# Fresh and reloaded keys mixed two and two, and half of a float split moved to VectorE, in a three-stage transformer block

## The chip, the cores and the metric

The kernel runs on one core of a Trainium2 chip. The time is the device time of one launch in microseconds, the median of several runs. The engines are named as the profile names them: PE is TensorE (PEld its weight loads), DVE is VectorE, ACT is ScalarE, POOL is GpSimd, SP is SyncE, which here only issues DMAs.

## What is computed

A mixing block of gated linear attention and spatial gating comes first. Then a retrieval layer takes most of the time: each of 1024 tokens picks 8 x 16 of 16384 single-neuron experts and sums them.

```python
def peer(x, w_q, sub_k1, sub_k2, expert_u, expert_v):
    q = (xt @ w_q).reshape(T, 8, 2, 128)
    s1 = einsum('thd,kd->thk', q[:, :, 0], sub_k1); s2 = einsum('thd,kd->thk', q[:, :, 1], sub_k2)
    v1, i1 = top_k(s1, 16); v2, i2 = top_k(s2, 16)
    cand = (v1[..., :, None] + v2[..., None, :]).reshape(T, 8, 256)
    vals, ci = top_k(cand, 16)
    idx = take(i1, ci // 16) * 128 + take(i2, ci % 16)
    gates = softmax(vals)
    ...
        u = expert_u[ii]                      # 128 rows of 1024 for each token
        a = gelu(einsum('tkd,td->tk', u, xx)) * gg
        return einsum('tk,tkd->td', a, expert_v[ii])
```

## The kernel before

The 1024 tokens are 8 blocks of 128. Blocks 0 to 3 fetch their experts row by row, with indirect DMAs that POOL issues: `u_steps` gathers rows of `expert_u` and a dot product on DVE (L748) takes each; `v_steps` (two of the blocks) sums rows of `expert_v` on PE into `gacc` (L828); `v_rows` (the other two) adds them up on DVE into `racc` (L799). Blocks 4 to 7 are computed densely: a *key* is a group of 128 experts, and for each of the 128 keys the hidden values of all 512 tokens are a matmul against `expert_u` (`h_phase`, `hp`), times a gate that is zero for most, and a second matmul against `expert_v` (`v_phase`, `vp`). Precision is kept by splitting each float into a high and a low half (`uh`/`ul`, `vh`/`vl`, `ah`/`al`) and three matmuls per product.

The program has four stages. **Stage 0** is the front block with top-k and its decoding (`topk_steps`). **Stage 1** is gateless: `h_phase` runs for the first HEAD = 72 keys and stores the results in DRAM (`a_d`), while `gate_steps` builds the gates of the dense blocks (`gJ`, `gW`, `gp`, `gst`) and stores them as `g_d`. **Stage 2** takes all 128 keys. For one of the first 72 the hidden values are reloaded (`Ar`); for one of the other 56 they are computed afresh. `gates` loads the gates `G` of G2 = 4 neighbouring keys at a time, `gated` multiplies and splits on DVE and ACT (L993 to L995), `split` loads `expert_u` or `expert_v` (`rawu`, `rawv`), makes the high half on ACT (L927) and the low half on DVE for `u` (L929) or on POOL for `v` (L931). After each group of GI = 4 keys one `v_phase` of 96 matmuls adds them to the sums `dacc` (DVE, L1011). It is recorded behind the first key of the next group. **The tail** is what is left of `v_rows`.

In stage 2 four fresh or four reloaded keys form a group, in the order RFRFRFRRFRFRFRFRRFRFRFRRFRFRFRFR (R reloaded, F fresh). Thus between two `v_phase`s lie four `h_phase`s, or one, or three, or, where reloaded groups meet, none.

Gathers are woven in by `Queue`: after each piece of matmul work `pump` gives a queue credit in proportion (rates 0.7 and 0.4 in stage 1, 0.65 and 0.4 in stage 2), and a gathered row costs 1.4. `paced` makes a gather wait for the last matmul recorded. A scheduler then sets the order of each engine's instructions, and every engine works in that order. A dot product is recorded UAHEAD rows behind its gather, 4 in stages 0 and 1 and 2 in stage 2; the gathered rows rotate through 5 buffers `gu` and, up to the end of stage 1, GUX = 4 more (`gux`).

Of the kernel before, what the change touches and what calls it, by code (L numbers as in the profile page):

```python
# [67 lines left out]
def block_kernel(ctx: ExitStack, tc: tile.TileContext, a, out):  # L68
# [518 lines left out]
    def topk_steps(b, G):  # L587
# [49 lines left out]
        nh = 2  # L637
        for h0 in range(0, HEADS, nh):
            hk = slice(h0 * TOPK, (h0 + nh) * TOPK)
            for half in range(2):  # L640
                eq = tk.tile([P, nh, TOPK, TOPK], BF16, name="eq")
                sh = [P, nh * TOPK, TOPK]
                nc.vector.tensor_tensor(eq.rearrange("p h k j -> p (h k) j"),
                                        ab[:, half, hk].unsqueeze(2).to_broadcast(sh),
                                        iota_f.unsqueeze(1).to_broadcast(sh), op=ALU.is_equal)
# [19 lines left out]
    def gate_steps(gb, b):  # L665
# [10 lines left out]
        def product():  # L676
# [235 lines left out]
    def dense(pump):  # L912
        TP = TB // 2 if TB > 512 else TB
        NP = TB // TP
        with tc.tile_pool(name="dn", bufs=1) as dn, ExitStack() as dvx:
# [193 lines left out]
```

## Time and profile before

| | us |
|---|---|
| median of three runs | 3422.1 (3421.41 to 3426.11) |
| the profiled execution | 3430.3 |
| its span, first to last instruction | 3428.4 |
| PE busy in it | 2960.9 (86%) |
| DVE busy | 2636.7 (77%) |
| POOL busy | 1915.4 (56%) |
| ACT busy | 1075.9 (31%) |

Stage 1 begins at 1174 us, the last matmul of stage 1 ends at 1872, stage 2's matmuls begin at 1899 and the last `dacc` sum ends at 3315. A matmul's record is longer than the step to the next one, since they are pipelined, so a busy PE is not a full one.

### The profile page before, as it was taken

The page shows a single profiled execution, that of the slowest core. Times are in us where ns is not written, and L with a number is a line of the kernel's source. Part 1 is how long each engine was busy: PE and PEld are TensorE (multiplying, and loading weights), DVE is VectorE, ACT ScalarE, POOL GpSimd, SP SyncE. Part 2 cuts the span into 40 slices and gives each one's busy share as a digit, 9 for nine tenths or more (in the row PEclk, how much of TensorE's full clock was granted, in tenths as well). Part 3 has the DMA queues.
Part 4 walks back from the last instruction along what each step waited for, and adds up shares of the span by engine and source line. Part 5 has one row for each costly group of instructions (what it writes and reads, how often), then busy time and mean ns, then how long its engine had stood idle before and what let it go on. Part 6 is the DMA issues. An engine that isn't in the chain of part 4 may idle for free. (4 is left out here: it accounts for less than half of the span.)

```text
span 3428.4 us, 42728 instructions
## 1 busy us (share of the span) xinstructions
PE 2960.9 (86%) x14906; PEld 2324.4 (68%) x14906; DVE 2636.7 (77%) x4989; ACT 1075.9 (31%) x2000; POOL 1915.4 (56%) x1303
## 2 busy tenths in 40 slices
PE   8988999998877799999898898999999988888840
PEld 8988888987867676676574565555655676666730
DVE  5656897789997797997865666565656688999999
ACT  5444233342323354555451221122111222222210
POOL 0002467655665364454455656676666666677776
PEclk9999899999988899999999899999999999989975
DMA  5555367764556698999899988988888878898888
GB/s 178 164 190 148 108 197 234 251 207 151 184 191 205 211 403 324 335 369 352 327 392 386 348 293 289 328 312 307 299 311 312 315 270 279 288 326 301 298 307 337
DMA packets 344442, 944.98 MB, mean 276 GB/s; under 512 B 32913, under 2 KB 123281, under 8 KB 342178
## 3 DMA queue, kind: packets, MB, share of 16 engines
q0 software_dynamic: 147456, 536.94, 43.1%
q1 hardware_dynamic: 196770, 405.31, 35.1%
q8 instruction: 117, 1.92, 0.2%
q14 instruction: 99, 0.81, 0.1%
HBM read 868.72 MB, written 73.40 MB: 275 GB/s over the span
## 5 line engine op out<-in xcount | busy, mean ns | idle before, releaser
L759 POOL DMA_INDIRECT gu<-in_pu,ii x370 | 448.3, 1212 | 374.0 <-PE hp L946 145.4
L246 POOL TENSOR_TENSOR wlo<-wraw,whi 128x1024 fp32r<-128x1024 f32 x140 | 351.5, 2528 | 482.7 <-ACT whi L244 475.6
L748 DVE SCALAR_TENSOR_TENSOR gu<-gu,gn 128x1024 f32<-128x1024 f32 x370 | 548.9, 1501 | 64.7 <-DMA gu<-in_pu,ii 63.9
L1007 PE MATMUL vp<-vl,ah 128*128 128x512 f32 x1024 | 422.6, 414 | 67.3 <-POOL vl L931 67.2
L1006 PE MATMUL vp<-vh,ah 128*128 128x512 f32 x1024 | 401.4, 418 | 76.3 <-ACT vh L927 45.4
L944 PE MATMUL hp<-dnh,uh 128*128 128x512 f32 x1024 | 411.2, 402 | 32.1 <-ACT uh L927 28.7
L1008 PE MATMUL vp<-vh,al 128*128 128x512 f32 x1024 | 414.0, 408 | 2.6 <-DVE al L995 2.6
L946 PE MATMUL hp<-dnh,ul 128*128 128x512 f32 x1024 | 408.0, 399 | 5.9 <-DVE ul L929 5.8
L945 PE MATMUL hp<-dnl,uh 128*128 128x512 f32 x1024 | 407.4, 398 | 0.0
L842 POOL DMA_INDIRECT gv<-in_pv,iT x256 | 292.4, 1142 | 203.3 <-PE gacc L828 112.2
L931 POOL TENSOR_TENSOR vl<-rawv,vh 128x1024 fp32r<-128x1024 f32 x128 | 328.5, 2578 | 70.6 <-ACT vh L927 69.2
L1011 DVE TENSOR_TENSOR dacc<-dacc,vp 128x512 f32<-128x512 f32 x256 | 169.2, 683 | 237.8 <-PE vp L1008 237.6
L244 ACT ACTIVATE whi<-wraw 128x1024 fp32r<-128x1024 f32 x216 | 225.3, 1057 | 287.1 <-DMA wraw<-in_wt 83.7
L828 PE MATMUL gacc<-gv,wz 128*32 128x512 f32 x1024 | 312.3, 603 | 2.9 <-DMA gv<-in_pv,iT 2.7
L1006 PEld LDWEIGHTS vp<-vh,ah 128*128 128x128 f32 x1024 | 202.5, 200 | 165.4 <-ACT vh L927 56.8
L1007 PEld LDWEIGHTS vp<-vl,ah 128*128 128x128 f32 x1024 | 203.0, 198 | 140.2 <-POOL vl L931 85.0
L759 POOL DMA_INDIRECT gux<-in_pu,ii x142 | 177.9, 1253 | 198.3 <-PE hp L946 89.6
L944 PEld LDWEIGHTS hp<-dnh,uh 128*128 128x128 f32 x1024 | 194.0, 190 | 110.0 <-ACT uh L927 32.7
L803 POOL DMA_INDIRECT gr<-in_pv,ii x151 | 192.3, 1273 | 101.1 <-DVE racc L799 61.8
L1008 PEld LDWEIGHTS vp<-vh,al 128*128 128x128 f32 x1024 | 202.7, 198 | 58.4 <-issue 12.6
L946 PEld LDWEIGHTS hp<-dnh,ul 128*128 128x128 f32 x1024 | 193.8, 189 | 69.1 <-issue 18.4
L945 PEld LDWEIGHTS hp<-dnl,uh 128*128 128x128 f32 x1024 | 194.2, 190 | 61.4 <-issue 23.5
(273 smaller groups left out, 6798.3 us busy)
## 6 DMA issues: line engine op xcount, KB each, us to landing
rawu<-in_ut SPq DMA_DIRECT2D x128, 512.0 KB, 7.0
rawv<-in_pv SPq DMA_DIRECT2D x128, 512.0 KB, 5.3
wraw<-in_wt SPq DMA_DIRECT2D x120, 512.0 KB, 3.9
g_d<-gst SPq DMA_DIRECT2D x16, 2048.0 KB, 11.0
G<-g_d SPq DMA_DIRECT2D x128, 256.0 KB, 8.0
wraw<-in_wq SPq DMA_DIRECT2D x48, 512.0 KB, 4.4
a_d<-A SPq DMA_DIRECT2D x72, 256.0 KB, 7.4
Ar<-a_d SPq DMA_DIRECT2D x72, 256.0 KB, 5.8
```

What stands on the lines that cost most here:

```text
L246: eng.tensor_tensor(lo[:, :, sl], raw, hi[:, :, sl].bitcast(F32), op=ALU.subtract)
L748: queued(nc.vector.scalar_tensor_tensor(u, u, 1.0, n2, op0=ALU.mult, op1=ALU.mult, accum_out=hv[:, k:k + 1]), "dve")
L759: paced(nc.gpsimd.indirect_dma_start(out=u, out_offset=None, in_=a["pu"], in_offset=bass.IndirectOffsetOnAxis(ap=ii[:, k:k + 1], axis=0)))
L828: queued(nc.tensor.matmul(acc[32 * g:32 * g + 32, dh, :], z[:, g, 31 - r:63 - r], v[:, dh * 512:(dh + 1) * 512], start=r == 0, stop=r == 3 ...
L842: paced(nc.gpsimd.indirect_dma_start(out=v, out_offset=None, in_=a["pv"], in_offset=bass.IndirectOffsetOnAxis(ap=iTs[b][:, t:t + 1], axis=0)))
L931: nc.gpsimd.tensor_tensor(lo, raw, hi.bitcast(F32), op=ALU.subtract)
L944: nc.tensor.matmul(ps[:, :TP], uh[:, cs], nh[:, c, ts_], start=c == 0, stop=False)
L945: nc.tensor.matmul(ps[:, :TP], uh[:, cs], nl[:, c, ts_], start=False, stop=False)
L946: mm = nc.tensor.matmul(ps[:, :TP], ul[:, cs], nh[:, c, ts_], start=False, stop=c == DC - 1)
L1006: nc.tensor.matmul(ps, ah[:, bl], vh[:, ds_], start=x == 0, stop=False)
L1007: nc.tensor.matmul(ps, ah[:, bl], vl[:, ds_], start=False, stop=False)
L1008: mm = nc.tensor.matmul(ps, al[:, bl], vh[:, ds_], start=False, stop=x == n - 1)
```

## The change

- `order`: a group of four keys in stage 2 is now two fresh and two reloaded ones, HEAD is 64 (so 64 keys are reloaded and 64 fresh), and between two `v_phase`s there are always two `h_phase`s.
- Gates: G2 = 2 keys to a load, 4 buffers; GT = 64 tokens to a stored tile, so `g_d` is written in 8 pieces of 4 MB and not 16 of 2 MB, and `gst` has 2 buffers, not 3.
- `vl` is computed on DVE. The raw tiles have two buffers each; those of `u` lie in the pool `dn`, which lives through both dense stages.
- GUX 1, UAHEAD (3, 2).
- Decoding: four heads at a time, with the 16 choices as the outer and the results as the inner dimension, in a buffer shared with `cd`.

```diff
-HEAD = 72
+HEAD = 64
-GT = 32
-G2 = 4
+GT = 64
+G2 = 2
-RAWB = {"h": 3, "u": 2, "v": 2}
+RAWB = 2
-GUX = 4
+GUX = 1
-UAHEAD = (4, 2)
+UAHEAD = (3, 2)
...
-        nh = 2
+        nh = 4
...
-                eq = tk.tile([P, nh, TOPK, TOPK], BF16, name="eq")
...
-                                        ab[:, half, hk].unsqueeze(2).to_broadcast(sh),
-                                        iota_f.unsqueeze(1).to_broadcast(sh), op=ALU.is_equal)
-                nc.vector.tensor_tensor(eq, eq, xi[:, half, hk].rearrange("p (h j) -> p h j", h=nh).unsqueeze(2)
-                                        .to_broadcast([P, nh, TOPK, TOPK]), op=ALU.mult)
...
+                eq = tk.tile([P, TOPK, nh * TOPK], BF16, name="eq", tag="cd")
+                sh = [P, TOPK, nh * TOPK]
+                nc.vector.tensor_tensor(eq, ab[:, half, hk].unsqueeze(1).to_broadcast(sh),
+                                        iota_f.unsqueeze(2).to_broadcast(sh), op=ALU.is_equal)
+                e4 = eq.rearrange("p j (h k) -> p j h k", h=nh)
+                nc.vector.tensor_tensor(e4, e4, xi[:, half, hk].rearrange("p (h j) -> p j h", h=nh).unsqueeze(3)
+                                        .to_broadcast([P, TOPK, nh, TOPK]), op=ALU.mult)
+                nc.vector.tensor_reduce(yz[:, half, hk], eq.rearrange("p j k -> p k j"), axis=AX.X, op=ALU.add)
...
-                raw = raws[dst].tile([P, D], F32, name="raw" + dst, bufs=RAWB["h" if raws["u"] is not raws.get("v") else dst])
+                raw = pool.tile([P, D], F32, name="raw" + dst, bufs=RAWB)
...
-                if dst == "u":
-                    last["dve"] = nc.vector.tensor_tensor(lo, raw, hi.bitcast(F32), op=ALU.subtract).ins
-                else:
-                    nc.gpsimd.tensor_tensor(lo, raw, hi.bitcast(F32), op=ALU.subtract)
+                last["dve"] = nc.vector.tensor_tensor(lo, raw, hi.bitcast(F32), op=ALU.subtract).ins
...
-                    G = dv.tile([P, NB, P // GT, G2, GT], F32, name="G", bufs=2)
+                    G = dv.tile([P, NB, P // GT, G2, GT], F32, name="G", bufs=4)
...
-            pairs = sorted(range(P // G2), key=lambda n: (n + 0.5) / HEAD if n * G2 < HEAD
-                           else (n - HEAD // G2 + 0.5) / (P - HEAD))
-            order = [n * G2 + x for n in pairs for x in range(G2)]
+            order = [i for n in range(0, HEAD, G2) for h in (HEAD, 0) for i in range(h + n, h + n + G2)]
```

**Where stage 2 begins, on SP.** `dacc` is the sum, loaded with `h`; its buffers lie where stages 0 and 1 had theirs, so the first of these loads waits for the last gather and dot of stage 1. Before:

```order
L975 DMA dacc3_17456<-h_d7_98 128x1024
L1022 DMA Ar_17461<-a_d0_11327 128x512
L983 DMA G_17463<-g_d4_131 128x4x128
L983 DMA G_17463<-g_d5_132 128x4x128
L983 DMA G_17463<-g_d6_133 128x4x128
L983 DMA G_17463<-g_d7_134 128x4x128
L926 DMA rawv_17475<-in_pv 128x1024
L1022 DMA Ar_17479<-a_d1_11328 128x512
L926 DMA rawv_17488<-in_pv 128x1024
L926 DMA rawu_17520<-in_ut 128x1024
```

and with the change:

```order
L957 DMA a_d63_11342<-A_16864 128x512
L924 DMA rawu_17079<-in_ut 128x1024
L924 DMA rawu_17313<-in_ut 128x1024
L969 DMA dacc0_16917<-h_d4_95 128x1024
L969 DMA dacc1_16918<-h_d5_96 128x1024
L969 DMA dacc2_16919<-h_d6_97 128x1024
L969 DMA dacc3_16920<-h_d7_98 128x1024
L977 DMA G_16971<-g_d4_131 128x2x128
L977 DMA G_16971<-g_d5_132 128x2x128
L977 DMA G_16971<-g_d6_133 128x2x128
L977 DMA G_16971<-g_d7_134 128x2x128
L924 DMA rawv_16983<-in_pv 128x1024
```

Two loads of `rawu` now stand ahead of the first `dacc`; the third stands 24 loads behind it. PE's order has 72 `hp` matmuls (three keys) ahead of the first `vp`, where before it had two matmuls.

**In stage 2, the low half of v.** Before, on POOL, among the gathers (`gv`, `gu`), from the middle of the stage:

```order
L931 TENSOR_TENSOR vl_19045<-rawv_19046,vh_19044 128x1024
L842 DMA gv_18912<-in_pv,iT_18226 128x1024
L842 DMA gv_18931<-in_pv,iT_18226 128x1024
L759 DMA gu_18564<-in_pu,ii_16144 128x1024
L931 TENSOR_TENSOR vl_19104<-rawv_19105,vh_19103 128x1024
L759 DMA gu_18567<-in_pu,ii_16144 128x1024
```

and with the change on DVE, from the end of one `v_phase` interval to the next:

```order
L926 TENSOR_TENSOR ul_19366<-rawu_19367,uh_19365 128x1024
L987 TENSOR_TENSOR A_19051<-A_19051,G_19089 128x512
L989 TENSOR_TENSOR al_19095<-A_19051,ah_19094 128x512
L926 TENSOR_TENSOR vl_19027<-rawv_19028,vh_19026 128x1024
L926 TENSOR_TENSOR vl_19040<-rawv_19041,vh_19039 128x1024
L748 SCALAR_TENSOR_TENSOR gu_18428,hv_16006<-gu_18428,gn2_16004 128x1024
L748 SCALAR_TENSOR_TENSOR gu_18431,hv_16006<-gu_18431,gn2_16004 128x1024
L1005 TENSOR_TENSOR dacc0_16917<-dacc0_16917,vp_19099 128x512
```

POOL keeps the gathers alone. On DVE the third and fourth `vl` of a group stand behind the gate of the next group's first fresh key (A, al) and, elsewhere, between dots.

**Where the dense work ends, on DVE.** The last `dacc` sum and what follows it, before:

```order
L1011 TENSOR_TENSOR dacc3_17456<-dacc3_17456,vp_26755 128x512
L149 SCALAR_TENSOR_TENSOR rfr_26631<-rfq_26635,rfr_26631 128x1
L145 SCALAR_TENSOR_TENSOR rfq_26683<-rfr_26679,rfh_26681 128x1
L799 SCALAR_TENSOR_TENSOR racc_24195<-gv_25112,w_24192,racc_24195 128x1024
L145 SCALAR_TENSOR_TENSOR rfq_26635<-rfr_26631,rfh_26633 128x1
```

and with the change:

```order
L1005 TENSOR_TENSOR dacc3_16920<-dacc3_16920,vp_26739 128x512
L799 SCALAR_TENSOR_TENSOR racc_24131<-gr_24183,w_24128,racc_24131 128x1024
L145 SCALAR_TENSOR_TENSOR rfq_26619<-rfr_26615,rfh_26617 128x1
L145 SCALAR_TENSOR_TENSOR rfq_26667<-rfr_26663,rfh_26665 128x1
L164 TENSOR_SCALAR rfv_26757<-rfss_26754 128x1
L799 SCALAR_TENSOR_TENSOR racc_24131<-gv_24200,w_24128,racc_24131 128x1024
```

Behind the last `dacc` sum stand 75 adds of `racc` before, and 124 now.

## Rows read from the trace of the kernel before

**Rows 1.** Busy time by stretch: us, each engine (count), PE clock, DMA share.
```profile
1174.00:1872.00 698.00, 667.75 (x3194) 468.30 (x3192) 573.62 (x1252) 345.13 (x828) 362.53 (x301) 0.98 0.94 355
1872.00:1899.00 27.00, 1.05 (x3) 0.81 (x4) 9.34 (x13) 4.21 (x5) 7.05 (x6) 0.58 0.99 335
1899.00:2684.00 785.00, 730.15 (x2854) 462.12 (x2853) 480.26 (x633) 157.61 (x235) 530.26 (x378) 0.96 0.89 311
2684.00:3315.00 631.00, 537.95 (x2164) 417.58 (x2162) 556.76 (x556) 140.86 (x195) 440.19 (x281) 0.93 0.85 294
3315.00:3428.40 113.40, 0.00 (x0) 0.00 (x0) 105.47 (x115) 1.72 (x6) 71.44 (x66) 0.51 0.88 342
```
**Rows 2.** What PE waited for, 1899 to 3315: us in total, times, longest.
```profile
PE vp L1007 <- POOL vl L931: 67.2, 31, 8.0
PE vp L1006 <- ACT vh L927: 45.4, 15, 8.3
PE vp L1006 <- DVE dacc L1011: 21.1, 13, 3.1
```
**Rows 3.** Groups on DVE, 1899 to 3315: count | busy us, mean ns | idle before.
```profile
L748 DVE SCALAR_TENSOR_TENSOR gu<-gu,gn 128x1024 f32<-128x1024 f32 x195 | 287.4, 1496 | 7.9 <-DMA gu<-in_pu,ii 7.3 <-DMA gn<-n_d 0.6
L799 DVE SCALAR_TENSOR_TENSOR racc<-gr,w,racc 128x1024 f32<-128x1024 f32 x114 | 180.7, 1585 | 4.7 <-DMA gr<-in_pv,ii 3.6
L1011 DVE TENSOR_TENSOR dacc<-dacc,vp 128x512 f32<-128x512 f32 x256 | 169.2, 683 | 237.8 <-PE vp L1008 237.6
L799 DVE SCALAR_TENSOR_TENSOR racc<-gv,w,racc 128x1024 f32<-128x1024 f32 x68 | 112.9, 1660 | 0.8
...
L995 DVE TENSOR_TENSOR al<-Ar,ah 128x512 fp32r<-128x512 f32 x70 | 76.7, 1097 | 30.2 <-ACT ah L994 29.2 <-PE vp L1007 0.9
```
**Rows 4.** Groups on POOL, 1899 to 3315.
```profile
L931 POOL TENSOR_TENSOR vl<-rawv,vh 128x1024 fp32r<-128x1024 f32 x127 | 326.0, 2578 | 51.5 <-ACT vh L927 50.1
```
**Rows 5.** Groups on DVE in stage 1, 1174 to 1872.
```profile
L748 DVE SCALAR_TENSOR_TENSOR gu<-gu,gn 128x1024 f32<-128x1024 f32 x108 | 129.7, 1217 | 12.2 <-DMA gu<-in_pu,ii 12.0
...
L692 DVE TENSOR_TENSOR gJ<-gT,iota_r 128x512 f32<-128x512 f32 x128 | 88.1, 688 | 62.0 <-PE gp L680 60.2 <-ACT gT L672 1.6
...
L929 DVE TENSOR_TENSOR ul<-rawu,uh 128x1024 fp32r<-128x1024 f32 x70 | 85.5, 1221 | 39.1 <-ACT uh L927 39.0
L643 DVE TENSOR_TENSOR eq<-ab,iota_f 128x512 bf16<-128x512 bf16 x24 | 16.6, 692 | 0.2
...
L646 DVE TENSOR_TENSOR eq<-eq,xi 128x512 bf16<-128x512 bf16 x24 | 10.2, 424 | 0.2
```
**Rows 6.** Groups on DVE in the tail, 3315 to 3428.4.
```profile
L799 DVE SCALAR_TENSOR_TENSOR racc<-gv,w,racc 128x1024 f32<-128x1024 f32 x38 | 48.8, 1284 | 1.1
```
**Rows 7.** PE in order of time: start us, us, instruction [idle before].
```profile
1897.95 0.80 PE L944 MATMUL hp<-dnh,uh 128*128 128x512 f32 x1 [26.54 <-ACT uh L927]
```
**Rows 8.** PE in order of time inside one v_phase.
```profile
2303.03 0.39 PE L1006 MATMUL vp<-vh,ah 128*128 128x512 f32 x1
...
2307.56 0.39 PE L1008 MATMUL vp<-vh,al 128*128 128x512 f32 x1
...
2309.43 0.40 PE L1008 MATMUL vp<-vh,al 128*128 128x512 f32 x1
2309.75 1.90 PE L828 MATMUL gacc<-gv,wz 128*32 128x512 f32 x8
...
2311.92 0.40 PE L1007 MATMUL vp<-vl,ah 128*128 128x512 f32 x1
```
**Rows 9.** SP in order of time where stage 2 begins.
```profile
1879.41 1.86 SPq L975 DMA_DIRECT2D dacc<-h_d  x4
...
1881.96 4.21 SPq L983 DMA_DIRECT2D G<-g_d  x4
```
**Rows 10.** DMA issues of the page: count, KB each, median us to landing.
```profile
rawu<-in_ut SPq DMA_DIRECT2D x128, 512.0 KB, 7.0
...
g_d<-gst SPq DMA_DIRECT2D x16, 2048.0 KB, 11.0
```

More of the change, by code (lines that the diff above doesn't have):

```diff
@@ L640, in topk_steps @@
             for half in range(2):
-                eq = tk.tile([P, nh, TOPK, TOPK], BF16, name="eq")
-                sh = [P, nh * TOPK, TOPK]
-                nc.vector.tensor_tensor(eq.rearrange("p h k j -> p (h k) j"),
-                                        ab[:, half, hk].unsqueeze(2).to_broadcast(sh),
-                                        iota_f.unsqueeze(1).to_broadcast(sh), op=ALU.is_equal)
-                nc.vector.tensor_tensor(eq, eq, xi[:, half, hk].rearrange("p (h j) -> p h j", h=nh).unsqueeze(2)
-                                        .to_broadcast([P, nh, TOPK, TOPK]), op=ALU.mult)
-                nc.vector.tensor_reduce(yz[:, half, hk], eq.rearrange("p h k j -> p (h k) j"), axis=AX.X,
-                                        op=ALU.add)
-                yield 1.8
+                eq = tk.tile([P, TOPK, nh * TOPK], BF16, name="eq", tag="cd")
[6 more added lines that the diff above has]
+                nc.vector.tensor_reduce(yz[:, half, hk], eq.rearrange("p j k -> p k j"), axis=AX.X, op=ALU.add)
+                yield 3.2
         if b in GB:
@@ L682, in product @@
             if t0 == 0:
-                st[0] = gb.tile([P, P, GT], F32, name="gst", bufs=3)
+                st[0] = gb.tile([P, P, GT], F32, name="gst", bufs=2)
             queued(nc.scalar.activation(st[0][:, :, t0:t0 + 4], ps.rearrange("p (t i) -> p i t", t=4), AF.Copy), "act")
@@ L917, in dense @@
             nl = dn.tile([P, DC, TB], F32R, name="dnl")
-            raws = {}
             def split(pool, dst, src):
@@ L953, in dense @@
             with tc.tile_pool(name="gb", bufs=1) as gb:
-                raws["u"] = gb
                 q_g = Queue(RATE_G)
@@ L957, in dense @@
                 for bb in range(NB):
-                    n2 = gb.tile([P, D], F32, name="dn2", tag="gst", bufs=3)
+                    n2 = gb.tile([P, D], F32, name="dn2", tag="gst", bufs=2)
                     nc.sync.dma_start(n2, n2_d[DB[bb]])
@@ L970, in dense @@
             q_u.rate, q_v.rate = RATE_U[2], RATE_V[2]
-            dv = raws["u"] = raws["v"] = dvx.enter_context(tc.tile_pool(name="dv", bufs=1))
+            dv = dvx.enter_context(tc.tile_pool(name="dv", bufs=1))
             acc = [dv.tile([P, D], F32, name=f"dacc{b}") for b in range(NB)]
@@ L1033, in dense @@
             v_phase(prev, lambda b: finish(dn, DB[b], acc[b], fg,
-                                           dv.tile([P, D], F32, name="fj", tag="rawu", bufs=RAWB["u"])))
+                                           dn.tile([P, D], F32, name="fj", tag="rawu", bufs=RAWB)))
     q_topk, q_u, q_v = Queue(RATE_TOPK), Queue(RATE_U[0]), Queue(RATE_V[0])
```

## Prediction

> **What bounds the kernel now.** I read first the busy times by stretch, which cut the span at 1174, 1872, 1899 and 3315 us [rows 1]. In stage 1 PE is busy for 667.75 of 698 us and DVE for 573.62: PE sets the pace, and there is some slack on DVE. Between 1872 and 1899 nothing runs on PE. In stage 2 PE is busy for 730 of 785 us at first, and from 2684 on for 538 of 631 while DVE is busy for 557: there the two engines bound each other. From 3315 to 3428 DVE alone works, 105 of 113 us. So four things are to be costed: PE's work and waits in stage 1, the hole, PE's waits in stage 2, and the rows left for the tail.
>
> Second come PE's waits in stage 2 [rows 2]. Three of them make 133.7 us: for `vl` from POOL 67.2, for `vh` from ACT 45.4, for a `dacc` sum on DVE 21.1. Third, the durations on DVE. The same dot takes 1217 ns in stage 1 [rows 5] and 1496 ns in stage 2 [rows 3]; the same add to `racc` takes 1284 ns in the tail [rows 6], 1585 and 1660 ns in stage 2; a subtraction of 128x512 is 1097 ns there (`al` from `Ar`), where one of the same size in stage 1 (`gJ`) is 688. What stage 2 has and the others don't have is `vl` on POOL, 127 x 2578 ns [rows 4]. The `dacc` sum, which reads one operand from PSUM, stays at 683 ns.
>
> The Trainium skill ("SBUF — State Buffer", "Who interferes with whom") says that a VectorE instruction with two inputs in SBUF and a GpSimd instruction that reads SBUF exclude each other, one blocking until the other has ended, and that one with a single SBUF input does not. The rows agree in all three kinds.
>
> **The low half of v on DVE.** It adds 128 subtractions of 128x1024. The price is that of `ul` without a neighbour on POOL, 1221 ns [rows 5]: 156 us. The blocking goes. I count it where a row with and one without are at hand: dots 195 x (1496 - 1217) = 54, adds 114 x (1585 - 1284) + 68 x (1660 - 1284) = 60, `al` 70 x (1097 - 688) = 29, in all 143 us, and the rest of `al`, `A` and `ul` on top. So DVE's load in stage 2 hardly changes, while POOL loses 326 us and issues its gathers without standing behind `vh`. `vl` no longer queues behind gathers that are paced by PE.
>
> **PE's waits in stage 2.** Two things act on the 133.7 us. A `vl` takes half as long and four of them no longer follow each other at 2.6 us. And between two `v_phase`s there are always two `h_phase`s. A matmul steps by 0.2265 us (20 steps from 2303.03 to 2307.56, [rows 8]), so a key's 24 take 5.44 us and two keys 10.9 us. In these 10.9 us the first `vh` and `vl` of the next group have to come; before it was none where reloaded groups meet. Against it stands that `vl` is now in the queue of DVE, behind dots, adds and the next key's gate. I take 15 for `vl`, 15 for `vh`, 11 for `dacc`: 41 us, 1.3 us for each of the 32 groups, so **-93 us**. The ends are 10 (nothing but a remainder) and all of the 133.7. PE's clock goes with this: it is 0.96 and 0.93 of full in the two stretches of stage 2 [rows 1], a loss of 0.04 x 785 + 0.07 x 631 = 75 us, and it is lowest where PE waited (0.58 in the hole). If most waits go I take a fifth of that back, **-15 us** (0 to -30).
>
> **Eight keys move from stage 1 to stage 2.** Stage 1 loses 8 x 5.44 = 43.5 us of PE, stage 2 gains them. In the built order 24 `gacc` matmuls move along. Four of them with two others take 2.49 us [rows 8], so one is 0.51 us and 24 are 12 us. Stage 1 **-56**, stage 2 **+56**. The stores of `g_d` become 4 MB. One of 2 MB lands after 11.0 us, a `rawu` of 512 KB after 7.0 [rows 10]; behind a store of 4 MB a load lands some 11 us later still. With two raw buffers, a `rawu` is issued about two keys before it must be split, and a key of stage 1 takes 698 / 72 = 9.7 us. So the cover is 19 us against 7 + 11 + some waiting. For eight stores I take 1.5 us each, **+12** (0 to 40: 5 us each).
>
> **The hole at 1872.** Before, PE waited 26.54 us [rows 7], since the loads of stage 2 wait for the buffers of stage 1 and even `rawu` is behind them. Now the first two fresh keys are loaded ahead and work for 10.9 us (counted above). But PE's third key stands ahead of the first `v_phase`, and its `rawu` behind 24 other loads. Before, `dacc` x4 took SP 1.86 us and `G` x4 4.21 us from 1879.41 on [rows 9]; at that pace the sixteen half-size `G` loads and the rest take SP 14 to 22 us, and then the load needs 7 us. PE's new wait is then some 16 to 25 us. I take **-8** (-20 to 0).
>
> **The tail.** The built order leaves 124 adds behind the last `dacc` and not 75. One costs at least DVE's 1.284 us [rows 6] and at most 113.4 / 75 = 1.51 [rows 1]; POOL is busy for 71 of 113 us there, so it is nearer to DVE's: 1.40 x 49 = **+69** (63 to 74).
>
> **The small edits.** Decoding has half as many instructions of twice the size. The Trainium skill ("VectorE: DVE Perf Modes", "Mode 2×_1P") asks for step ±1 in all tensors for its double rate with 16-bit data; the change gives the multiplication a broadcast as the innermost dimension, which its operands didn't have. The rows fit: the comparison, which has such a broadcast, takes 692 ns for 512 elements, the multiplication 424 [rows 5]. By the rule 64 x 0.27 = 17 us of DVE are added, over stages 0 and 1, and without it nothing. By the rows alone the edit lies between a saving of some fixed time per instruction and a multiplication that is as slow as the comparison; 124 us of DVE are idle in stage 1 alone, so it is hidden there. A lookahead of 3 rows and not 4 lets DVE wait more for gathers (12.2 us for 108 dots in stage 1 now), and one buffer less holds up the transposes where stage 1 begins. For all this **+8** (0 to 25). The 128 KB loads of `G` carry the same bytes in twice as many issues, SP has room: nothing; if that fails, it shows as waits of DVE for `G`.
>
> **Sum**, against the profiled execution (3430.3 us, span 3428.4): -93 - 15 - 56 + 12 + 56 - 8 + 69 + 8 = -27, so 3403. That execution lies 8.2 us over the median of 3422.1; the forecast for the median is **3395**.
>
> **The rivals.** *First, the waits change hands (slower).* Every engine works in order; `vl` three and four stand behind the next key's gate and behind dots that wait for a gather, and from 2684 on DVE has 557 busy us of 631 [rows 1]. Without the -93 and the -15 the sum is +81: if PE waits as long for DVE as it did for POOL, the time is 3503. It decides from 134 - 81 = 53 us of remaining waits on, 1.7 us per group. For it: DVE's load does not fall. Against it: 10.9 us of cover at every group. I think of 3430 to 3500. *Second, the waits go wholly (faster).* Waits 10, clock -30, the tail at its lower end, no cost of stores: -124 - 30 - 56 + 0 + 56 - 15 + 63 + 0 = -106, so 3316. For it: POOL's delays were behind two of the three waits. *Third, stage 1 pays (slower).* The stores at 40 and the small edits at 25 add 45 us to the forecast: 3440. For it: two buffers and 11 us more; against it: PE waited next to nothing there. That the change doesn't do what it says is excluded, since the order shows `vl` on DVE and the keys mixed.
>
> **How the numbers follow.** The forecast's own range is 3370 to 3425, with a chance of 0.45. The first rival has 0.30, the second (3316 to 3370) 0.17, the third 0.08. About 0.2% of the time, 7 us, is what a measurement can tell from no change. Of the forecast 0.38 is faster by more than this; with the second rival that makes 0.55. Of the forecast's upper end and the first rival's lower one 0.13 lie within 7 us of 3422. The other 0.32 is slower. The range that leaves out 2 in 10 is 3330 to 3465.
>
> **What would show it.** Right: dots of stage 2 near 1217 ns and adds near 1284; PE's waits for `vl`, `vh` and `dacc` well under 60 us; the last `dacc` some 90 us earlier than 3315; a tail of about 180 us and not 113; a wait of PE shortly after stage 1. Wrong: PE waiting for `vl` on DVE for over 2 us in each group, stage 1 ending later than 1835, or dots that stay at 1.5 us.

## The result, and the profile after

The changed kernel takes 3367.4 us (median of 4 runs, 3363.6 to 3379.6), the kernel before, on the same chip, 3424.1 (4 runs, 3421.4 to 3430.4): a ratio of 0.9838 with a 95% interval of 0.9809 to 0.9867, so 57 us or 1.6% less. The profiled execution took 3365.84 us.

The busy times by stretch, for the stretches that answer to [rows 1]: from, to, length, then busy us and count of PE, PEld, DVE, ACT and POOL, PE clock, DMA share, GB/s.

```profile
1181.00:1845.00 664.00, 613.74 (x2948) 431.55 (x2946) 544.37 (x1159) 334.37 (x810) 334.95 (x268) 0.97 0.90 338
1845.00:1880.00 35.00, 24.56 (x95) 14.36 (x94) 18.78 (x28) 7.59 (x11) 18.56 (x16) 0.93 1.03 398
1880.00:2658.00 778.00, 755.23 (x2948) 469.34 (x2949) 471.13 (x695) 164.20 (x245) 371.62 (x310) 0.98 0.90 317
2658.00:3186.00 528.00, 516.31 (x2224) 412.23 (x2222) 478.91 (x607) 143.57 (x199) 259.87 (x193) 1.00 0.92 325
3186.00:3364.00 178.00, 0.00 (x0) 0.00 (x0) 168.47 (x167) 1.72 (x6) 119.42 (x116) 0.51 0.93 362
```

Five milestones cut the span into stretches that add up: the first product of stage 1, the start of the last one of a gateless key, the first product of stage 2 into `vp`, the last `dacc` sum, and the end.

| stretch | before | after | difference |
|---|---|---|---|
| stage 0 | 1174.6 | 1181.4 | +6.8 |
| stage 1 | 694.6 | 662.3 | -32.3 |
| to the first `vp` | 29.8 | 36.5 | +6.7 |
| to the last `dacc` | 1416.0 | 1305.8 | -110.2 |
| tail | 113.4 | 178.0 | +64.6 |
| span | 3428.4 | 3364.1 | -64.3 |

What PE waited for from 1880 to 3186 us (us in total, times, longest), against [rows 2]:

```profile
PE vp L1000 <- ACT vh L925: 28.0, 9, 9.5
PE vp L1000 <- DVE dacc L1005: 5.6, 3, 3.8
PE vp L1001 <- DVE vl L926: 3.4, 2, 3.2
PE vp L1000 <- ACT ah L988: 2.4, 2, 1.7
```

The groups on DVE in the same stretch (count | busy us, mean ns | idle before), against [rows 3, 4], and the adds of the tail, against [rows 6]:

```profile
L748 DVE SCALAR_TENSOR_TENSOR gu<-gu,gn 128x1024 f32<-128x1024 f32 x212 | 254.8, 1218 | 3.7 <-DMA gu<-in_pu,ii 3.6
...
L926 DVE TENSOR_TENSOR vl<-rawv,vh 128x1024 fp32r<-128x1024 f32 x128 | 154.9, 1219 | 72.1 <-ACT vh L925 68.9 <-DMA G<-g_d 3.1
L799 DVE SCALAR_TENSOR_TENSOR racc<-gr,w,racc 128x1024 f32<-128x1024 f32 x88 | 112.5, 1278 | 1.9 <-DMA gr<-in_pv,ii 1.5
```
```profile
L799 DVE SCALAR_TENSOR_TENSOR racc<-gv,w,racc 128x1024 f32<-128x1024 f32 x62 | 79.6, 1284 | 2.0
L799 DVE SCALAR_TENSOR_TENSOR racc<-gr,w,racc 128x1024 f32<-128x1024 f32 x62 | 79.6, 1284 | 2.0
```

To be read here: the dots are back from 1496 to 1218 ns and the adds from 1585 and 1660 to 1278, the wait for `vl` has gone from 67.2 to 3.4 us, and PE is busy for 516 of 528 us at full clock in the last part of stage 2, where it was 538 of 631. Of the 28.0 us for `vh` 8.7 are the wait at the very start, which belongs to the stretch before. The tail has grown by 65 us: it is 124 adds of 1284 ns, and was 75.

### The profile page after: what moved, and what is told of

The parts are those of the page before. It is cut to its first block, busy times and chain, and to the rows that moved or that the text cites. A ratio compares the mean times of both kernels' runs of the same rounds, so it can differ in the third digit from the quotient of the medians.

```text
span 3364.1 us, 42653 instructions
## 1 busy us (share of the span) xinstructions
PE 2931.7 (87%) x14906; PEld 2302.8 (68%) x14906; DVE 2595.4 (77%) x5021; ACT 1079.0 (32%) x2000; POOL 1616.2 (48%) x1175
## 4 chain that ended last, share of the span: by engine, by line
PE 33%; DVE 9%; DMA 5%; issue 3%; POOL 1%; ACT 1%; SPq 0%; DVEq 0%; POOLq 0%; ACTq 0%
PE gacc L828 6%; PE vp L1001 6%; PE vp L1000 6%; PE vp L1002 6%; DVE racc L799 5%; PE hp L941 3%; PE hp L939 3%; PE hp L940 3%; DMA rawv<-in_pv 1%; DMA Ar<-a_d 1%; DMA G<-g_d 1%; DVE vl L926 1%; DMA gv<-in_pv,ii 1%; POOL gu L759 1%; DMA gv<-in_pv,iT 1%
## 5 line engine op out<-in xcount | busy, mean ns | idle before, releaser
L759 POOL DMA_INDIRECT gu<-in_pu,ii x463 | 578.8, 1250 | 662.8 <-DVE gu L748 219.7
L748 DVE SCALAR_TENSOR_TENSOR gu<-gu,gn 128x1024 f32<-128x1024 f32 x463 | 631.1, 1376 | 94.9 <-DMA gu<-in_pu,ii 94.4
L842 POOL DMA_INDIRECT gv<-in_pv,iT x256 | 306.6, 1198 | 295.7 <-PE gacc L828 181.0
L1000 PE MATMUL vp<-vh,ah 128*128 128x512 f32 x1024 | 388.0, 400 | 37.0 <-ACT vh L925 28.0
L1001 PE MATMUL vp<-vl,ah 128*128 128x512 f32 x1024 | 405.5, 397 | 3.6 <-DVE vl L926 3.4
L1002 PE MATMUL vp<-vh,al 128*128 128x512 f32 x1024 | 394.8, 395 | 1.4 <-DVE al L989 1.4
L828 PE MATMUL gacc<-gv,wz 128*32 128x512 f32 x1024 | 329.3, 603 | 1.5 <-DMA gv<-in_pv,iT 1.4
L926 DVE TENSOR_TENSOR ul<-rawu,uh 128x1024 fp32r<-128x1024 f32 x128 | 156.1, 1220 | 117.9 <-ACT uh L925 97.8
L803 POOL DMA_INDIRECT gr<-in_pv,ii x149 | 179.2, 1203 | 140.7 <-DVE racc L799 88.9
L925 ACT ACTIVATE vh<-rawv 128x1024 fp32r<-128x1024 f32 x128 | 131.1, 1051 | 320.7 <-PE vp L1002 284.8
```

What stands on the lines that cost most here:

```text
L748: queued(nc.vector.scalar_tensor_tensor(u, u, 1.0, n2, op0=ALU.mult, op1=ALU.mult, accum_out=hv[:, k:k + 1]), "dve")
L759: paced(nc.gpsimd.indirect_dma_start(out=u, out_offset=None, in_=a["pu"], in_offset=bass.IndirectOffsetOnAxis(ap=ii[:, k:k + 1], axis=0)))
L828: queued(nc.tensor.matmul(acc[32 * g:32 * g + 32, dh, :], z[:, g, 31 - r:63 - r], v[:, dh * 512:(dh + 1) * 512], start=r == 0, stop=r == 3 ...
L842: paced(nc.gpsimd.indirect_dma_start(out=v, out_offset=None, in_=a["pv"], in_offset=bass.IndirectOffsetOnAxis(ap=iTs[b][:, t:t + 1], axis=0)))
L1000: nc.tensor.matmul(ps, ah[:, bl], vh[:, ds_], start=x == 0, stop=False)
L1001: nc.tensor.matmul(ps, ah[:, bl], vl[:, ds_], start=False, stop=False)
```

## Experiments: which part of the change makes the gain

Two theories. A: the gain comes from `vl` leaving POOL; the order of the keys only helps or hinders. B: it comes from the two fresh keys between reloaded ones, which cover the first `vh` and `vl` of the next group.

**The change without the move of `vl`.**

```diff
-    last["dve"] = nc.vector.tensor_tensor(lo, raw, hi.bitcast(F32), op=ALU.subtract).ins
+    if dst == "u":
+        last["dve"] = nc.vector.tensor_tensor(lo, raw, hi.bitcast(F32), op=ALU.subtract).ins
+    else:
+        nc.gpsimd.tensor_tensor(lo, raw, hi.bitcast(F32), op=ALU.subtract)
```

> The changed kernel with the low half of v on GpSimd again; all else stays. Theory A (the move of vl makes the gain): dots in stage 2 go from 1218 ns back to about 1.5 us, adds of racc from 1278 ns to about 1.6 us, TensorE waits again for vl, 60 us or more in stage 2, and for vh; most of the gain of 57 us goes, 3400 to 3430 us. Theory B (mixing fresh and reloaded keys makes the gain, by its cover of two hp keys between v_phases): dots slow down too, but TensorE's waits stay under 50 us in all, and the time stays under 3390 us. The tail is shorter than 178 us in both if the order leaves fewer adds behind.

Measured: 3494.1 us, ratio 1.0188 (1.0168 to 1.0208), far above the 3400 to 3430 that theory A gave. The wait for `vl` and the long dots and adds of [rows 2, 3] are there again, with the mixed order (waits of PE and groups on DVE, 1887 to 3324 us):

```profile
PE vp L1004 <- POOL vl L929: 67.3, 31, 6.3
...
L748 DVE SCALAR_TENSOR_TENSOR gu<-gu,gn 128x1024 f32<-128x1024 f32 x212 | 290.9, 1393 | 10.8 <-DMA gu<-in_pu,ii 10.6 <-issue 0.2
L799 DVE SCALAR_TENSOR_TENSOR racc<-gr,w,racc 128x1024 f32<-128x1024 f32 x95 | 164.6, 1733 | 4.1 <-DMA gr<-in_pv,ii 3.5
```

The wait for `vl` on POOL is as long as before the change (67.3 against 67.2 us), so two fresh keys of cover did not shorten it; the one for `vh` is half as long (22.7 against 45.4). Stage 2 takes 1437 us, 131 more than in the changed kernel. B falls: without the move the rest of the change makes the kernel 1.9% slower.

**The move of `vl` alone, in the kernel before.** The same line, the other way round: `split` puts both low halves on VectorE, nothing else is changed.

> The kernel before with vl on VectorE and nothing else. Theory A: dots at 1218 ns and adds at 1.28 us in stage 2, the 67 us of waiting for vl nearly gone, the waits for vh smaller; stage 2 is shorter by 60 us or more, the tail longer than 113 us as VectorE carries 156 us more in the order; 3370 to 3400 us. Theory B: the waits only move to VectorE's queue, since reloaded groups still meet without a cover; TensorE's waits stay over 100 us and the time within 15 us of 3424.

Measured: 3326.4 us, 0.9695 (0.9668 to 0.9721), 103 us less than before and 41 less than the whole change, and better than theory A's 3370 to 3400. (The kernel before took 3424.1 us beside the changed kernel and 3429.3 to 3429.8 beside the runs of these sections, so a difference between a run here and the changed kernel is good to some 6 us: taken from the two ratios the 41 would be 49.) Its stage 2 begins at the same 1899.0 us as before. The stretch to the last `dacc` and then the tail:

```profile
1899.00:3183.90 1284.90, 1231.08 (x5017) 857.68 (x5015) 955.24 (x1291) 299.84 (x430) 636.14 (x509) 0.99 0.92 325
3183.90:3327.50 143.60, 0.00 (x0) 0.00 (x0) 134.89 (x138) 1.59 (x6) 95.23 (x89) 0.51 0.91 354
```
```profile
PE vp L1003 <- ACT vh L927: 26.5, 13, 4.5
PE vp L1003 <- DVE dacc L1008: 16.2, 12, 3.9
PE vp L1004 <- DVE vl L928: 7.0, 6, 2.6
```

Stage 2 falls from 1416 to 1285 us, and `vl` on DVE keeps PE waiting for 7 us although four reloaded keys still follow each other. This is the cleanest measure of the blocking. DVE was busy for 480.26 + 556.76 = 1037 us of stage 2 [rows 1]; now 955, with 153 us of `vl` added and 23 adds fewer (29 us). So the 326 us of `vl` on POOL [rows 4] had stretched DVE's other work by 1037.0 - 955.2 + 153.0 - 29.4 = 205 us. The Trainium skill ("SBUF — State Buffer", "Who interferes with whom") states the exclusion; that it costs DVE more than the moved work itself is what this run adds. That POOL, relieved, issues its gathers earlier is not the cause: in stage 2 DVE's dots waited 7.3 us for gathered rows before [rows 3] and wait 7.4 now.

The trace of the kernel before shows the same instruction by instruction. Stage 2 has 683 dots, adds, gate products and subtractions on DVE. Of these 134 overlap a `vl` on POOL in time and last 2.54 us on average; the other 549 last as long as without POOL (dots 1217 ns, adds 1280). What the 134 last longer than the others of their kind makes 193 us, close to the 205. So the 1496 ns of [rows 3] is the duration of hardly any dot: most take 1217 ns, and some wait out one `vl` or, as here, two:

```profile
2271.58 4.75 POOL L931 TENSOR_TENSOR vl<-rawv,vh 128x1024 fp32r<-128x1024 f32 x2
2272.25 5.17 DVE L748 SCALAR_TENSOR_TENSOR gu<-gu,gn 128x1024 f32<-128x1024 f32 x1
```

**The mix alone, in the kernel before, with `vl` left on POOL.**

```diff
-HEAD = 72
-G2 = 4
+HEAD = 64
+G2 = 2
-G = dv.tile([P, NB, P // GT, G2, GT], F32, name="G", bufs=2)
+G = dv.tile([P, NB, P // GT, G2, GT], F32, name="G", bufs=4)
-order = [n * G2 + x for n in pairs for x in range(G2)]
+order = [i for n in range(0, HEAD, G2) for h in (HEAD, 0) for i in range(h + n, h + n + G2)]
```

> The kernel before with 64 keys in the gateless stage, two fresh and two reloaded keys to a group and gates loaded for two; vl stays on GpSimd, stores of g_d stay at 2 MB, decoding, lookahead and buffers as before. Theory A: vl on GpSimd goes on slowing VectorE (dots about 1.5 us) and TensorE waits for it 60 us or more; 3405 to 3430 us. Theory B: the waits for vh and vl fall from 113 to under 50 us, and the time to under 3390 us.

Measured: 3506.1 us, 1.0214 (1.0192 to 1.0236). PE's waits in stage 2:

```profile
PE vp L1007 <- POOL vl L931: 104.0, 28, 9.6
PE vp L1006 <- DVE dacc L1011: 22.0, 9, 4.0
PE vp L1006 <- ACT vh L927: 19.3, 11, 3.7
```

The wait for `vh` gets shorter (45.4 to 19.3 us) and the one for `vl` longer (67.2 to 104.0): with POOL in the way, the mix loses 77 us (3429.6 for the kernel before in this comparison), and the time lies above what either theory expected. The loss is not in PE's waits, which are 152 us where they were 146. Stage 1 gets 62 us shorter and stage 2, which takes over its keys, 65 longer; but the stretch between them grows by 15 us and the tail by 63, since 124 adds are left for it and not 75.

**Four fresh and four reloaded keys, in the changed kernel.** Gates are still loaded for two.

```diff
-order = [i for n in range(0, HEAD, G2) for h in (HEAD, 0) for i in range(h + n, h + n + G2)]
+order = [i for n in range(0, HEAD, 4) for h in (HEAD, 0) for i in range(h + n, h + n + 4)]
```

> The changed kernel with groups of four fresh and of four reloaded keys in turn, fresh first; vl stays on VectorE, 64 keys in the gateless stage. Between two v_phases there are now one and three hp keys in turn, not two. Theory A: TensorE's waits in stage 2 stay under 70 us (41 us now) and the time within 15 us of the changed kernel's 3367. Theory B: waits for vh and vl of over 100 us return, since a cover of 5.4 us is too short for four splits, and the time is over 3410 us.

Measured: 3366.6 us, 0.9806 (0.9784 to 0.9828): no difference from the change. But it comes about otherwise: stage 2 takes 1334 us instead of 1306, PE waits 59 us in it instead of 33, and the tail takes 153 instead of 178, since 105 adds are left for it and not 124. What one stretch gains the other gives back: DVE's adds have to be done somewhere, and how many of them the built order puts behind the last `dacc` is part of what a variant costs.

## Experiments: what gives back 41 us

Theory: the small edits of stages 0 and 1. Rival: the mix and the 64 keys.

**The mix with `vl` on VectorE, without the small edits.** The edit is that of the mix alone, above, together with the move of `vl`.

> The kernel before with the low halves of v on VectorE, 64 keys in the gateless stage, and two fresh keys alternating with two reloaded ones (gates loaded for two); the decoding, the gate stores of 2 MB, the buffers and the lookahead of u stay as before. It stands between the run with the low halves on VectorE alone (3326.4 us) and the whole change (3367.4 us), and divides the 41 us between them. If the small edits of stages 0 and 1 hold them (the first product starts at 1181 instead of 1175 us, stage 1 takes 662 instead of about 634 us for 64 keys): 3325 to 3345 us, the first product of stage 2 near 1853 us, as in the mixed run with POOL (1853.6), and the last product into dacc near 3160. If the mix and the 64 keys hold them: 3355 to 3380 us, with stage 2 longer than the 1306 us of the changed kernel or the tail longer than its 178 us.

Measured: 3342.7 us, 0.9746 (0.9719 to 0.9772). So of the 41 us the mix holds 16 and the small edits 25. The mix's 16 are a trade again: the matmuls of eight keys and 62 `gacc` have left stage 1, 40 of these for stage 2, which takes only 1294 us instead of 1285 (PE at 1.00 of its clock), but the tail takes 201.5 us instead of 143.6, with 133 adds instead of 98. Here the cover does help: PE waits 23 us in stage 2, where the move alone left 51.

```profile
PE vp L1004 <- DVE vl L928: 11.5, 7, 2.8
PE vp L1003 <- ACT vh L927: 10.9, 9, 1.4
```

The small edits are in stage 0 (1170.6 against 1181.4), in stage 1 (630.2 against 662.3) and in stage 2 (1294 against 1306), less the 24 us that they save in the tail and 7 in front of stage 2.

**Gate stores of 2 MB in the changed kernel.**

```diff
-GT = 64
+GT = 32
-st[0] = gb.tile([P, P, GT], F32, name="gst", bufs=2)
+st[0] = gb.tile([P, P, GT], F32, name="gst", bufs=3)
-n2 = gb.tile([P, D], F32, name="dn2", tag="gst", bufs=2)
+n2 = gb.tile([P, D], F32, name="dn2", tag="gst", bufs=3)
```

> The changed kernel with the gate matrix stored in pieces of 2 MB from three buffers, as before, instead of 4 MB from two. The prediction put the larger stores at 12 us of stage 1. If they are what makes stage 1 slow in the changed kernel (662.2 us for 64 keys, 634 in the run that keeps the old edits): stage 1 takes 635 to 645 us and the time is 3340 to 3355 us. If not: stage 1 stays at 655 to 665 us and the time within 6 us of 3367 us.

Measured: 3389.7 us, 0.9877 (0.9850 to 0.9904), 22 us slower than the change (13 by the ratios), which neither case expected, and stage 1 takes 666.5 us, no less. The large stores do not cost stage 1 anything; undoing them costs 4 to 8 us in each of the five stretches. Why was not settled: the edit also halves the runs that the loads of `G` read, and stage 0, which it does not touch, is 4 us longer too.

**The old decoding in the changed kernel.** The block of the diff that computes `eq` is put back (two heads at a time, choices not innermost), in one buffer.

```diff
-        nh = 4
+        nh = 2
-                eq = tk.tile([P, TOPK, nh * TOPK], BF16, name="eq", tag="cd")
+                eq = tk.tile([P, nh, TOPK, TOPK], BF16, name="eq", tag="cd")
...
-                nc.vector.tensor_reduce(yz[:, half, hk], eq.rearrange("p j k -> p k j"), axis=AX.X, op=ALU.add)
+                nc.vector.tensor_reduce(yz[:, half, hk], eq.rearrange("p h k j -> p (h k) j"), axis=AX.X,
+                                        op=ALU.add)
```

> The changed kernel with the decoding of before: two heads at a time, the choices in an inner axis per key, instead of four heads with the choices innermost. The prediction gave the new decoding no cost or gain of its own beyond the 8 us of the small edits. If the new decoding delays the end of stage 0 (first product at 1181.4 us against 1174.6 before): the first product returns to about 1175 us and the time falls by 4 to 8 us. If the new decoding is a gain that something else hides: the first product comes later than 1181 us and the time is 3370 to 3385 us. If it is neutral: within 5 us of 3367 us.

Measured: 3359.8 us, 0.9797 (0.9768 to 0.9825), 7.6 us less (14 by the ratios, whose intervals overlap); the first product of stage 1 is back at 1169.8 us. The decoding in the kernel before (stages 0 and 1):

```profile
L643 DVE TENSOR_TENSOR eq<-ab,iota_f 128x512 bf16<-128x512 bf16 x64 | 63.5, 992 | 0.3
L646 DVE TENSOR_TENSOR eq<-eq,xi 128x512 bf16<-128x512 bf16 x64 | 43.3, 677 | 0.3
L648 DVE TENSOR_REDUCE ij<-eq 128x32 f32<-128x512 bf16 x32 | 21.7, 679 | 0.4
L648 DVE TENSOR_REDUCE yz<-eq 128x32 f32<-128x512 bf16 x32 | 21.4, 670 | 0.0
```

and in the changed one:

```profile
L644 DVE TENSOR_TENSOR eq<-ab,iota_f 128x1024 bf16<-128x1024 bf16 x32 | 48.0, 1501 | 0.1
L647 DVE TENSOR_TENSOR eq<-eq,xi 128x1024 bf16<-128x1024 bf16 x32 | 42.0, 1314 | 0.1
L649 DVE TENSOR_REDUCE yz<-eq 128x64 f32<-128x1024 bf16 x16 | 31.9, 1994 | 0.0
L649 DVE TENSOR_REDUCE ij<-eq 128x64 f32<-128x1024 bf16 x16 | 31.0, 1936 | 0.1
```

The comparison gains 15.5 us and the sum over the choices loses 19.8: it now runs across the rows of `eq`, and twice the elements take not twice but three times as long (1994 ns against 670). The multiplication comes to the same in all, 42.0 against 43.3 us, but its own price has risen. In stage 1, where POOL only issues gathers, one takes 1220 ns, as long as the comparison (1217) and more than twice the 424 of [rows 5]. In stage 0 POOL computes low halves of weights (`wlo`). Before, 30 of the 40 multiplications there overlap none of these and take 411 ns, and the other ten take 2085 on average; in the change 15 of 20 take 1209 ns, and the other five 1856. At the prices without POOL the multiplications cost 12 us more than before, and the comparison saves 5 us and not 15.5; the rest is that fewer of them fell on a `wlo`. The sums, which read one tensor, last as long beside a `wlo` as without (669 and 671 ns before). The Trainium skill ("VectorE: DVE Perf Modes", "Mode 2×_1P"), by which the prediction would have added 17 us to the multiplication, fits the rows of both stages; the total hides it.

**The lookahead of u alone,** put into the mix with `vl` on VectorE (3342.7 us).

```diff
-GUX = 4
+GUX = 1
-UAHEAD = (4, 2)
+UAHEAD = (3, 2)
```

> The mixed kernel with the low halves of v on VectorE and the small edits left as before (3342.7 us), with one small edit put in: the lookahead of the gathered u rows as in the changed kernel (one extra buffer instead of four, three rows ahead instead of four). Together the small edits cost 25 us between that kernel and the changed one (3367.4), 7.6 of which the old decoding gives back. If the lookahead holds most of the other 17 us: 3355 to 3362 us, with the first product of stage 1 after 1174 us or stage 1 over 640 us (630 before for 64 keys). If it holds nothing: within 5 us of 3343 us.

Measured: 3365.9 us, 0.9820 (0.9797 to 0.9843), 23 us more and above the expected range, but not where it was expected: stage 1 takes 618.4 us, 12 less. It is paid behind it: PE waits 41.4 us in one piece for the first fresh key's `uh` (17.0 without the edit), and the tail is 220 us long, with 148 adds.

**The raw buffers alone,** put into the same kernel: two each in the common pool.

```diff
-RAWB = {"h": 3, "u": 2, "v": 2}
+RAWB = 2
-raw = raws[dst].tile([P, D], F32, name="raw" + dst, bufs=RAWB["h" if raws["u"] is not raws.get("v") else dst])
+raw = pool.tile([P, D], F32, name="raw" + dst, bufs=RAWB)
```

> The mixed kernel with the low halves of v on VectorE and the small edits left as before (3342.7 us), with one small edit put in: two buffers each for the raw keys of u and v in the common pool, in place of three in stage 1 and a pool of their own. If the buffers make stage 1 slow (two raw keys instead of three: the next load waits for ACT's uh and VectorE's ul): stage 1 takes 645 to 660 us instead of 630, the waits of TensorE for uh and ul in it come back (33 us in the changed kernel, 30 in this one's base), the hole behind it is nearly gone, since fresh keys are loaded ahead, and the time is 3350 to 3362 us. If not: stage 1 at 630 us and the time 3330 to 3345 us, lower by what the hole gives.

Measured: 3381.9 us, 0.9861 (0.9836 to 0.9886), 39 us more, twice what was expected. Stage 1 takes 669.2 us, and the stretch behind it 33.6 instead of 43.6, since the fresh keys' loads no longer wait for a buffer of stage 1.

**The third raw buffer alone.** Two buffers in stage 1 in their old pool.

```diff
-RAWB = {"h": 3, "u": 2, "v": 2}
+RAWB = {"h": 2, "u": 2, "v": 2}
```

> The mixed kernel with the low halves of v on VectorE and the small edits left as before (3342.7 us), with two buffers for the raw keys of u in stage 1 instead of three, in their old pools. The move of the raw buffers to two each in the common pool cost 39 us (3381.9), 39 of it in stage 1 (669 instead of 630 us). If the third buffer is what stage 1 lives on: stage 1 takes 655 to 670 us and the time is 3365 to 3385 us. If it is the common pool (which lets loads of v and of the next keys start earlier and takes room from others) and not the number: stage 1 stays at 628 to 638 us and the time within 8 us of 3343 us.

Measured: 3360.4 us, 0.9798 (0.9782 to 0.9815), 18 us more; stage 1 takes 661.7 us, 31 more, of which the stretches behind it give back 11. So it is the number that stage 1 feels; the common pool adds some 8 us there. Stage 1 with three buffers, and with two, as busy times, and what PE waits for in the latter:

```profile
1170.60:1800.80 630.20, 603.33 (x2926) 429.62 (x2926) 534.05 (x1192) 330.98 (x806) 322.10 (x262) 0.98 0.93 351
```
```profile
1173.60:1835.20 661.60, 621.82 (x2942) 436.06 (x2942) 534.83 (x1197) 332.41 (x806) 309.50 (x266) 0.98 0.89 338
```
```profile
PE hp L941 <- ACT uh L927: 22.1, 16, 4.0
PE hp L943 <- DVE ul L928: 14.0, 14, 3.5
```

With three, the same waits are 2.1 and 4.2 us. How a buffer that is only an entrance makes PE wait is seen in SP's queue. The same part of it with three and with two, in the order of the program:

```
518 L960 DMA a_d25_11352<-A_14121 128x512
519 L926 DMA rawu_14695<-in_ut 128x1024
520 L926 DMA rawu_14783<-in_ut 128x1024
521 L960 DMA a_d26_11353<-A_14216 128x512
```
```
526 L960 DMA a_d29_11356<-A_14451 128x512
527 L926 DMA rawu_14695<-in_ut 128x1024
528 L926 DMA rawu_14783<-in_ut 128x1024
529 L960 DMA a_d30_11357<-A_14544 128x512
```

The same two loads stand behind the store of key 25 with three buffers and behind that of key 29 with two, and a store waits for its key's `A`. SP's waits in stage 1, with three:

```profile
SPq L926 <- DVE ul L928: 208.6, 36, 18.0
SPq L960 <- ACT A L945: 78.6, 22, 7.1
```

and with two:

```profile
SPq L960 <- ACT A L945: 297.8, 54, 12.6
SPq L926 <- DVE ul L928: 140.2, 43, 10.6
```

The loads now follow PE instead of running ahead of it; ACT and DVE split a key when PE already wants it.

The small edits, each measured alone (decoding and stores by taking them out of the change, the others by putting them into the mix), do not add up: 7.6 + 23 + 39 - 22 = 48 us, and together they cost 25. The common pool removes the hole that the shorter lookahead makes longer, which would be part of it; that was not tried.

## Experiments: the adds of the tail

Theory: DVE has room for the tail's adds earlier. Rival: wherever they are put, they push back what PE waits for. Both kernels are the one before with `vl` on VectorE (3326.4 us).

```diff
-RATE_U = (0.35, 0.7, 0.65)
+RATE_U = (0.5, 0.7, 0.65)
```

> The kernel before with the low halves of v on VectorE, and the adds and dots of the u steps issued faster in stage 0 (rate 0.5 instead of 0.35), which leaves 43 adds behind the last product into dacc instead of 98. It tests whether the tail's adds, 1.28 us each, can be moved to where VectorE waits. If they find free time in stage 0: the tail falls from 144 us by 55 adds, 70 us, to about 75 us, and the time to 3260 to 3280 us. If stage 0 lengthens by as much as the tail falls (they stand ahead of the scores and the decoding on VectorE): the first product of stage 1 comes 60 us later, at about 1235 us, and the time stays within 10 us of 3326 us.

Measured: 3310.3 us, 0.9648 (0.9619 to 0.9677), the fastest version of all, 3.5% under the kernel before.

```diff
-RATE_U = (0.35, 0.7, 0.65)
+RATE_U = (0.35, 0.9, 0.8)
```

> The kernel before with the low halves of v on VectorE (3326.4 us), and the adds and dots of the u steps issued faster in the stages behind stage 0 (rates 0.9 and 0.8 instead of 0.7 and 0.65), which leaves 54 adds behind the last product into dacc instead of 98. In stage 0 the same shift of 55 adds took 70 us off the tail and put 52 us on stage 0, to 3310.3 us. If VectorE has free time in stages 1 and 2 beside TensorE: the tail falls by 44 adds, 56 us, and the time to 3270 to 3290 us. If TensorE waits there for VectorE's ul and vl as much as the tail falls: 3310 to 3330 us, with the waits for ul in stage 1 above 30 us instead of 5.

Measured: 3325.3 us, 0.9709 (0.9683 to 0.9734). Stages 0 and 1, and the tail, of the first of the two:

```profile
0.00:1224.50 1224.50, 1032.14 (x6699) 977.33 (x6699) 966.91 (x2534) 427.39 (x735) 573.70 (x326) 0.92 0.62 202
1224.50:1916.90 692.40, 668.78 (x3190) 465.50 (x3190) 568.65 (x1245) 345.08 (x826) 371.19 (x302) 0.99 0.94 358
...
3234.60:3306.00 71.40, 0.00 (x0) 0.00 (x0) 64.27 (x84) 1.77 (x6) 37.30 (x34) 0.52 0.79 301
```

The rate is that of the gathers for dots. In the first kernel 53 more dots run in stage 0, the adds can begin earlier in stage 2, and 43 of them are left instead of 98: that takes 72 us off the tail and puts 52 on stage 0, between the two cases expected. In the second 51 more dots run in stage 1 and 54 adds are left: that takes 58 us off the tail and puts 26 on stage 1, 7 on the hole and 20 on stage 2, so nothing is left. So the rival's time came. The wait it named did not: PE waits 2.4 us for `ul` in stage 1 of the second kernel. What grew there is this (PE's waits and ACT's, 1172.5 to 1895.3 us):

```profile
PE hp L941 <- ACT A L945: 19.1, 13, 4.9
PE gtp L670 <- DVE ij L648: 11.2, 4, 7.3
```
```profile
ACT A L945 <- DMA a_d<-A: 15.6, 4, 7.0
```

Without the edit these are 3.3, 4.3 and 0.6 us. ACT's `A` waits for the store of an earlier one, which stands in SP's queue among loads that wait for DVE's `ul` (243.7 us with the edit, 204.2 without). DVE is idle for 124 of 698 us in stage 1 [rows 1], and a dot there is still not free: by these waits its delay goes round by SP and ACT to PE.

## Why the prediction was right, and where not

The forecast was 27 us less, 57 was measured. The sign is right, and so is the mechanism of the gain: the end of the blocking and of PE's waits for `vl`. The time lies inside the range that leaves out 2 in 10 (3330 to 3465), but 3 us below the forecast's own (3370 to 3425), since most of the misses go one way. The gain that the prediction expected of the whole change comes from the move of `vl` alone (3326); the mix, which it counted as a help, and the small edits give back 41 us. By its steps:

- **DVE's load** (right, and understated). "DVE's load in stage 2 hardly changes": 1037 before, 950 after. The 143 us counted from dots, adds and `al` were 205 by the run with `vl` alone moved.
- **PE's waits, -93** (right, and understated). The forecast left 15 for `vl`, 15 for `vh` and 11 for `dacc`, 41 us; the waits after are 3.4, 28.0 and 5.6, with `ah` and smaller ones 42, of which 8.7 belong to the hole. So all waits in stage 2 fell from 146 to 33, by 113 us. The reason given was half wrong: it is POOL's absence that shortens them first, and the two fresh keys only then. Moving `vl` alone leaves 51 us, the mix with it 23, and mixing alone 152.
- **The clock, -15** (mis-sized). Stage 2 ran at 0.98 and 1.00 after 0.96 and 0.93. PE was busy in it for 1268 us before and 1272 after, but with 120 `hp` and 32 `gacc` more, some 38 us, so 35 us came back. The run with `vl` alone moved shows it with the same products: 5018 kept PE busy for 1268 us, and now 5017 for 1231, so 37 us. "A fifth" of the 75 should have been half. With the waits this makes most of the 43 us by which the stretch from the last gateless product to the last `dacc` beat the forecast (-103 against -93 - 15 + 56 - 8 = -60): 20 are the waits of stage 2, some 20 the clock and 8 the hole, against a little more work than counted.
- **The hole, -8** (miscounted). PE's waits there fell from 26.5 to 10.5 us, by 16 and so twice as much. The two loads of `rawu` that stand behind the last store of stage 1 in SP's order are not those of the first two fresh keys but of the third and the fourth: SP issues 68 loads of `rawu` ahead of the first `dacc`, and stage 1 has 64 keys. So three keys run before the first `v_phase`, and PE's wait in front of it is 8.74 us for `vh`, not 16 to 25 for a `rawu`:

```profile
1847.06 3.76 SPq L924 DMA_DIRECT2D rawu<-in_ut  x2
1852.82 1.76 SPq L969 DMA_DIRECT2D dacc<-h_d  x4
1854.62 4.07 SPq L977 DMA_DIRECT2D G<-g_d  x4
```
```profile
1880.15 0.80 PE L1000 MATMUL vp<-vh,ah 128*128 128x512 f32 x1 [8.74 <-ACT vh L925]
```

- **Stage 1, -56 + 12** (the cost was mis-sized, and its cause was another). It fell by 32 us and ended at 1844, behind the 1835 that the prediction itself had named as a sign of being wrong. The 56 are about right by luck, since two errors cancel: the 2.49 us of [rows 8] hold eight `gacc` and not four, and 49 of them went along by the traces (418 in stage 1 before, 369 after) and not 24. By the steps around them one costs 0.31 us in stage 1, so the work that left is 43.5 + 49 x 0.31 = 59 us and the cost some 26 instead of 12. It is not the stores (2 MB stores leave stage 1 at 666 us) but the third raw buffer, 31 us of stage 1 by itself. The prediction computed a cover of 19 us for two buffers, from the issue of a load; it did not look at what stands ahead of the load in SP's queue. PE's waits for `ul` and `uh` in stage 1 are 19.3 and 12.2 us, and were 5.8 and 2.1.
- **The tail, +69** (right): +64.6, at 1.32 us for each of 49 adds, nearer to DVE's 1.284 than taken. The move alone leaves 98 adds, the mix with it 133.
- **The small edits, +8** (right in size for stage 0 in these two traces: +6.8). Over all kernels with the same rates in stage 0 the first product comes at 1170 to 1179 us with the old decoding (nine traces) and at 1181 to 1188 with the new (four), some 12 us apart. The sum over a strided axis, which the prediction did not name, costs DVE 20 us; the multiplication, which it did, costs 12 that the total hides. With stage 1's +12 the forecast put 20 us on what the small edits cost, and 25 were measured, but for other reasons: that is luck.
- **The rivals.** The first asked for more than 53 us of waits left; 33 are. With `vl` put back on POOL the time came to 3494, near its 3503, but there PE waits for POOL and not, as it said, for DVE. The second's 3316 is near what the move of `vl` gives without the rest (3326), but by other terms: 51 us of waits are left there, and the tail grows by only 30. The third happened in part: the small edits cost 25 us, though not by the stores.

## What to carry to other kernels

Before an elementwise step is put on POOL to relieve DVE, compare the durations of DVE's two-input work in a stretch with POOL running and one without: here 326 us on POOL cost DVE 205, and taking 128 steps back shortened DVE's stage. Where an engine that ends last carries work that can be put off, a change to the stage in front of it also changes how much is left for the end (here 43 to 148 adds, at 1.3 us each); follow the count of deferred steps and not one stage's time. A staging buffer is worth the place of its load in the issuing queue: look up which stores, and whose results, stand ahead of it.

## What was not expected of the hardware

The price of sharing was larger than the moved work: 1.6 us of DVE for each 2.58 us `vl` on POOL, against 1.22 us for the same subtraction on DVE. A reduction over the outer axis took 1994 ns for 1024 elements, where 512 along the inner axis took 670. And PE's clock moved with waits of some microseconds. It was 0.96 and 0.93 of full in the two parts of stage 2 in which PE idled for 55 and 93 us; with 23 and 12 us of idling it was 0.98 and 1.00, the level of 2.4 GHz but for one stretch of 3.4 us at 1.2. In the run with `vl` alone moved the waits fell by 94 us, and the clock gave back 37 more.
